# The output group's products in another order, and one product's weights summed ten half slabs sooner

## The chip, the cores and the metric

The kernel runs on one core of a Trainium2 chip. The metric is the device time of one execution in microseconds (us). It is given as the median of several runs; beside them one execution was taken by the hardware profiler, and every duration below is from that one. Engines are named as the profile names them: PE is TensorE, PEld its weight loads, ACT ScalarE, DVE VectorE, POOL GpSimd, SP SyncE.

## The reference, cut to what matters

Two layers over 256 tokens and a model width of 2048, all in fp32. Each layer normalises, projects into four branches (sparse attention, retention, a gated recurrence, attention into a memory), multiplies each branch's output by a gate, sums the four, and projects the sum with `w_out` into the residual:

```python
def hybrid_layer(x, mem, norm_g, w_in, qk_g, ...):
    h = rms_norm(x, norm_g)
    u = h @ w_in
    ...
    merged = jnp.zeros_like(x)
    for n, (y, z) in enumerate(((y_a, a_z), (y_b, b_z), (y_c, c_z), (y_m, m_z))):
        branch = y.reshape(B, S, W).astype(dt) * jax.nn.silu(z)
        merged = merged + jax.nn.sigmoid(gate_all[:, :, n]) * (branch @ w_branch[n])
    return x + merged @ w_out
```

The change concerns the last product, `merged @ w_out`, of the second layer: 256 x 2048 by 2048 x 2048. It is called the output group below.

## The kernel before

**Matrix products in parts.** Each fp32 operand is split into a high and a low part in a format that TensorE takes at full rate, and a product is made of three: high by high, high by low, low by high. Names that end in h and l are such parts (mg0h, mg0l); `whi` and `wlo` are those of the weights. A matmul of the GEMMs is 128 x 128 by 128 x 512, recorded at L145 for all of them; the other operations of ACT, DVE and POOL are recorded at L127, so the lines of the profile go by tile names.

**Weight slabs.** Weights come in slabs of 1 MB (128 x 2048), which SP loads into `raw` (four buffers; `load`, L420). Each slab is cut into two half slabs: `cut_piece` makes `whi` with a cast on ACT and then `wlo` with a subtraction on DVE. There are four buffers of such pairs, so the cuts run four half slabs ahead of PE: each time PE has been given the matmuls of one half slab, `advance` cuts another, and first sends what is due for later ones. An ordinary half slab of an output block feeds 12 matmuls.

**The merged rows.** `merged` is held in four column blocks acc0 to acc3. Each is turned by a transpose on DVE and 16 small DMAs (`mgp<-mgpi`), which POOL and SP issue in turns; those of acc1, which comes last, are all on POOL. Then ACT and DVE make mg0h and mg0l, and so on. The blocks are done in the order 0, 3, 2, 1 (`MERGED`), which are blocks 0, 1, 2, 3 of the output group.

**The output group of the last layer.** `w_out` is taken in four column chunks of 512. Chunks 0 and 1 are made block by block (tile `wo`): (c, b) in `LAST_ORDER` is block b of chunk c, one slab, two half slabs, 24 matmuls. Chunks 2 and 3 are made together, as a two by two scheme over both halves of rows and columns with seven products in place of eight (tile `px`). A plain number i in `LAST_ORDER` is such a product: four half slabs of 6 matmuls each. `last_take` makes one and `last_forms` makes the row combinations that four of them need: s3 for product 1, s1 for 3, s2 for 4, r4 for 0 (each is split into h and l on ACT and DVE). Products 2, 5 and 6 take merged rows as they are.

The weights of products 0 and 5 are raw slabs. Those of the others are sums of blocks of `w_out`, which DMAs make: a first block is loaded by SP (`last_block`, L494), and further ones are added onto it by accumulating DMAs that POOL issues. There are two chains of four half slabs. Chain y (`sumy`) serves products 2, 3, 4 and 6 one after another: as a half slab has been cut for one product, the next block is added onto it for the next (`LAST_NEXT`). Chain x (`sumx`) serves product 1 alone: one load and one accumulate for each half slab. `LAST_BEGIN` says how many half slabs ahead of a product's first cut its loads and accumulates are sent, in units of `AHEAD` = 10; `last_product` in `gemm_plan` turns this into positions in the list of cuts, and `split_weights` sends them when the cuts come to that position.

**What sets the order.** Each engine works through its instructions in the order in which the program issues them, and that order comes from the list of cuts: the combinations, casts and copies are tasks that get their turns between cuts. POOL's and SP's DMA queues have eight completion lanes each, so that a DMA waits for the one eight before it on its queue.

Of the kernel before, what the change touches and what calls it, by code (L numbers as in the profile page):

```python
# [154 lines left out]
DUO, AHEAD, FIRST, MERGED = (2, 0, 3, 1), 10, 0, (0, 3, 2, 1)  # L155
# [1 line left out]
STAGES = ((False, 1, 1), (True, 0, 1), (False, 0, 0), (True, 0, 1), (True, 1, 1))  # L157
LAST_SUM, RING, EARLY = (True, 1, 0), 5, 8
BETWEEN_PRODUCTS = (4, 3, 4, 4, 3, 2, 3)
LAST_ORDER = ((0, 0), (1, 0), (0, 1), (1, 1), 2, (0, 2), 1, (1, 2), 3, (0, 3), 4, 0, (1, 3), 5, 6)  # L160
LAST_RAW, LAST_NEXT = {0: (1, 1), 5: (1, 0)}, {2: (True, 0, 1), 3: (True, 1, 1), 4: (True, 1, 0)}
LAST_BEGIN = {2: ((AHEAD, "y", (False, 0, 0)),), 1: ((2 * AHEAD, "x", (False, 0, 1)), (AHEAD, "x", (True, 1, 1)))}
MOVES, STEPS, BANKS, WARM = 5, 2, 2, 7
MARGIN, LATE = 500.0, 2500.0

# [123 lines left out]
def gemm_plan(wmem, win, wbr, wout):  # L289
# [22 lines left out]
    def last_product(l, i, part):  # L312
# [3 lines left out]
        if not part:  # L316
            for ahead, chain, stage in LAST_BEGIN.get(i, ()):
                begins[len(cuts) - ahead] = chain, stage
# [5 lines left out]
    for l in range(L):  # L324
# [18 lines left out]
        if l + 1 < L:  # L343
# [3 lines left out]
            continue  # L347
        for at in LAST_ORDER:
            if isinstance(at, tuple):
# [14 lines left out]
def trunk(ctx: ExitStack, tc: tile.TileContext, x, xt, memt, ng, qkg, hg, lbl, win, wmem, wbr, wout,  # L364
# [1251 lines left out]

    for at in LAST_ORDER:
        if isinstance(at, tuple):
# [61 lines left out]
```

## Time and profile before

| what | us |
|---|---|
| median of 3 runs | 1836.58 |
| the runs | 1834.44, 1836.58, 1836.6 |
| the profiled execution | 1835.12 |
| its span, first to last instruction | 1833.3 |
| PE busy in the span | 1801.6 |
| DVE, ACT, POOL busy in the span | 1369.4, 1077.8, 400.6 |

The profiled execution lies 1.5 below the median of the runs, and its span 1.8 below its own time. The output group begins at 1716.04 us of the span with block (0, 0), and PE's last matmul ends about 10 us before the span does.

How to read the rows: a row of the timeline has the start in us from the span's start, the busy time, the engine, the line, the operation, the tile written, the tiles read, their shape, how many instructions the row joins (x4), and in brackets how long the engine was idle before it and what ended that. For a DMA row on POOL or SP the time is that of the issue; when a transfer lands is in the chain of waits, which gives issue and duration until landing, and in the views by tile. A row of the view by windows gives for a stretch each engine's busy time and number of instructions, the granted TensorE clock (1.00 is full speed), the busy share of the DMA engines and GB/s.

### The profile page before, as it was taken

What the parts mean: (1) busy time and instruction counts of PE and PEld (TensorE: products, weight loads), DVE (VectorE), ACT (ScalarE), POOL (GpSimd) and SP (SyncE); (2) the same over time, 40 slices, a digit from 0 to 9 for tenths busy, and PEclk for the clock granted to TensorE, in tenths of its full rate; (3) what the DMA queues carried; (4) which work ended last, traced back from release to release, by engine and by line L of the source; (5) the groups of instructions that cost most, each with busy time, mean ns of one, the idle gap of its engine ahead of it and who ended that gap; (6) DMA issues with size and microseconds to landing.
All of it is one profiled execution on the core that took longest, in us unless ns stands there. A gap on an engine that the chain in (4) does not pass through costs nothing.

```text
span 1833.3 us, 24392 instructions
## 1 busy us (share of the span) xinstructions
PE 1801.6 (98%) x8812; PEld 1497.3 (82%) x8812; DVE 1369.4 (75%) x1482; ACT 1077.8 (59%) x1283; POOL 400.6 (22%) x599
## 2 busy tenths in 40 slices
PE   9999999999999999999999999999999999999976
PEld 8889888888888888888888888888888888888854
DVE  5667798787878677777566698787877868677665
ACT  5756665456767656564466656545666755655453
POOL 0022420033332110103231340004322211111320
PEclk9999999999999999999999999999999999999988
DMA  8769965689999899977785985669999999996986
GB/s 333 267 208 307 276 213 197 235 240 266 282 268 285 258 237 284 248 236 240 244 273 184 308 238 194 225 227 258 258 287 249 290 257 270 261 247 226 300 192 167
DMA packets 127401, 459.84 MB, mean 251 GB/s; under 512 B 23472, under 2 KB 44720, under 8 KB 95024
## 3 DMA queue, kind: packets, MB, share of 16 engines
q1 hardware_dynamic: 89200, 356.14, 55.6%
q0 software_dynamic: 37792, 101.88, 28.7%
q8 instruction: 69, 1.13, 0.2%
q14 instruction: 52, 0.43, 0.1%
q10 hardware_dynamic: 288, 0.26, 0.0%
HBM read 428.05 MB, written 6.29 MB: 237 GB/s over the span
## 4 chain that ended last, share of the span: by engine, by line
PE 94%; DMA 4%; DVE 0%; ACT 0%; issue 0%; SPq 0%; POOL 0%; ACTq 0%; POOLq 0%
PE u L145 50%; PE px L145 22%; PE bw L145 9%; PE wo L145 6%; PE mv L145 2%; PE mk L145 2%; DMA sumy<-in_wout 1%; DMA mgp<-mgpi 1%; DMA raw<-in_wout 1%; PE ixrp L145 0%; PE mov L145 0%; PE mlg L145 0%; PE co L145 0%; PE bo L145 0%; PE aov L145 0%
## 5 line engine op out<-in xcount | busy, mean ns | idle before, releaser
L127 DVE TENSOR_TENSOR wlo<-raw,whi 128x1024 fp32r<-128x1024 f32 (+3 forms) x548 | 645.2, 1186 | 314.3 <-ACT whi L127 309.3
L127 ACT CAST whi<-raw 128x1024 fp32r<-128x1024 f32 (+3 forms) x548 | 559.3, 1024 | 536.7 <-PE u L145 339.3
L127 DVE TENSOR_TENSOR wlo<-sum,whi 128x1024 fp32r<-128x1024 f32 x240 | 288.0, 1220 | 63.8 <-ACT whi L127 57.1
L127 ACT CAST whi<-sum 128x1024 fp32r<-128x1024 f32 x240 | 250.5, 1053 | 101.2 <-PE px L145 50.7
L127 POOL DMA_DIRECT2D sum<-in_win x152 | 137.3, 910 | 609.3 <-DVE wlo L127 575.1
L127 POOL DMA_DIRECT2D mgp<-mgpi x72 | 38.4, 549 | 152.1 <-issue 94.0
L145 PE MATMUL u<-whi,x11h 128*128 128x512 f32 (+2 forms) x176 | 67.5, 384 | 0.0
L145 PE MATMUL u<-whi,x01h 128*128 128x512 f32 (+2 forms) x176 | 67.5, 384 | 0.0
L145 PE MATMUL u<-whi,x02h 128*128 128x512 f32 (+2 forms) x176 | 67.5, 383 | 0.0
L145 PE MATMUL u<-whi,x12h 128*128 128x512 f32 (+2 forms) x176 | 67.4, 383 | 0.0
L145 PE MATMUL u<-whi,x00h 128*128 128x512 f32 (+2 forms) x176 | 67.4, 383 | 0.0
L145 PE MATMUL u<-whi,x10h 128*128 128x512 f32 (+2 forms) x176 | 67.4, 383 | 0.0
L145 PE MATMUL u<-whi,x13h 128*128 128x512 f32 (+2 forms) x176 | 67.2, 382 | 0.0
L145 PE MATMUL u<-whi,x03h 128*128 128x512 f32 (+2 forms) x176 | 67.1, 381 | 0.0
L145 PE MATMUL u<-wlo,x11h 128*128 128x512 f32 (+2 forms) x176 | 67.1, 381 | 0.0
L145 PE MATMUL u<-wlo,x01h 128*128 128x512 f32 (+2 forms) x176 | 67.1, 381 | 0.0
L145 PE MATMUL u<-wlo,x00h 128*128 128x512 f32 (+2 forms) x176 | 67.1, 381 | 0.0
L145 PE MATMUL u<-wlo,x02h 128*128 128x512 f32 (+2 forms) x176 | 67.1, 381 | 0.0
L145 PE MATMUL u<-whi,x10l 128*128 128x512 f32 (+2 forms) x176 | 67.1, 381 | 0.0
L145 PE MATMUL u<-wlo,x12h 128*128 128x512 f32 (+2 forms) x176 | 67.0, 381 | 0.0
L145 PE MATMUL u<-wlo,x03h 128*128 128x512 f32 (+2 forms) x176 | 67.0, 381 | 0.0
L145 PE MATMUL u<-wlo,x10h 128*128 128x512 f32 (+2 forms) x176 | 67.0, 381 | 0.0
(536 smaller groups left out, 4594.9 us busy)
## 6 DMA issues: line engine op xcount, KB each, us to landing
raw<-in_win SPq DMA_DIRECT2D x180, 1024.0 KB, 6.6
sum<-in_win POOLq DMA_DIRECT2D x152, 512.0 KB, 8.6
sum<-in_win SPq DMA_DIRECT2D x80, 512.0 KB, 6.9
raw<-in_wbr SPq DMA_DIRECT2D x32, 1024.0 KB, 6.9
raw<-in_wout SPq DMA_DIRECT2D x28, 1024.0 KB, 6.7
raw<-in_wmem SPq DMA_DIRECT2D x12, 1024.0 KB, 5.3
sumy<-in_wout POOLq DMA_DIRECT2D x12, 512.0 KB, 10.4
raw<-in_win SPq DMA_DIRECT2D x8, 656.0 KB, 4.3
```

Of the source, the lines that this page charges most:

```text
L127: return call(*args, **kw)
L145: return self.engine.matmul(out, w, x, **kw)
```

## The change

Two lines differ. `LAST_ORDER` puts product 2 ahead of block (1, 1) and product 3 ahead of block (1, 2); from product 4 on it is as before. Between products 2 and 3 of chain y stand (1, 1), (0, 2) and product 1, where (0, 2), product 1 and (1, 2) stood; between 3 and 4 stand (1, 2) and (0, 3), where (0, 3) stood alone. `LAST_BEGIN` sends the loads of chain x 30 half slabs ahead of product 1's first cut in place of 20, and the accumulates 20 ahead in place of 10.

```diff
-LAST_ORDER = ((0, 0), (1, 0), (0, 1), (1, 1), 2, (0, 2), 1, (1, 2), 3, (0, 3), 4, 0, (1, 3), 5, 6)
+LAST_ORDER = ((0, 0), (1, 0), (0, 1), 2, (1, 1), (0, 2), 1, 3, (1, 2), (0, 3), 4, 0, (1, 3), 5, 6)
 LAST_RAW, LAST_NEXT = {0: (1, 1), 5: (1, 0)}, {2: (True, 0, 1), 3: (True, 1, 1), 4: (True, 1, 0)}
-LAST_BEGIN = {2: ((AHEAD, "y", (False, 0, 0)),), 1: ((2 * AHEAD, "x", (False, 0, 1)), (AHEAD, "x", (True, 1, 1)))}
+LAST_BEGIN = {2: ((AHEAD, "y", (False, 0, 0)),), 1: ((3 * AHEAD, "x", (False, 0, 1)), (2 * AHEAD, "x", (True, 1, 1)))}
```

On the engines this moves the following. POOL's queue, from the last of the earlier sums to the end of the output group's accumulates (`mgp<-mgpi` are the transposes of the merged rows, eight for each of acc0, acc3 and acc2 and sixteen for acc1; `sumx` and `sumy` are the accumulates of the two chains):

```order
 L127 DMA sum<-in_win 128x1024 x32
-L127 DMA mgp<-mgpi 32x2x128 x28
+L127 DMA mgp<-mgpi 32x2x128 x2
 L127 DMA sumx<-in_wout 128x1024 x4
-L127 DMA mgp<-mgpi 32x2x128 x12
-L127 DMA sumy<-in_wout 128x1024 x12
+L127 DMA mgp<-mgpi 32x2x128 x36
+L127 DMA sumy<-in_wout 128x1024
+L127 DMA mgp<-mgpi 32x2x128 x2
+L127 DMA sumy<-in_wout 128x1024 x11
```

The four accumulates of chain x stood behind 28 of the 40 transposes, among acc1's; they stand now behind the first two of acc0's. The first accumulate of chain y stands ahead of the last two of acc1's.

ACT from mg3h on, before (s3h is the combination for product 1, `us` the copy of product 2's result; `whi<-raw` and `whi<-sumy` are cuts):

```order
L127 CAST mg3h<-mgp 128x1024
L127 CAST whi<-raw 128x1024 x3
L127 CAST s3h<-r_14522 128x1024
L127 CAST whi<-sumy 128x1024 x2
L127 CAST mg2h<-mgp 128x1024
L127 CAST mg1h<-mgp 128x1024
```

and in the changed kernel:

```order
L127 CAST mg3h<-mgp 128x1024
L127 CAST whi<-raw 128x1024
L127 CAST whi<-sumy 128x1024 x2
L127 CAST s3h<-r_14522 128x1024
L127 CAST whi<-sumy 128x1024 x2
L127 CAST whi<-raw 128x1024
L127 CAST mg2h<-mgp 128x1024
L127 CAST whi<-raw 128x1024 x3
L127 COPY us<-px 128x512
L127 CAST mg1h<-mgp 128x1024
```

Between mg3h and mg1h stood five cuts; now there are nine and the copy of product 2's result.

ACT at the cuts of product 0 and the cast of its combination r4h, before:

```order
L127 CAST whi<-sumy 128x1024 x2
L127 COPY xc<-wo 128x512 x2
L127 CAST whi<-raw 128x1024
L127 CAST r4h<-r_14522 128x1024
L127 CAST whi<-raw 128x1024 x7
```

and in the changed kernel:

```order
L127 CAST whi<-sumy 128x1024 x3
L127 COPY xc<-wo 128x512 x2
L127 CAST whi<-raw 128x1024 x4
L127 CAST r4h<-r_14522 128x1024
L127 CAST whi<-raw 128x1024 x4
```

DVE at the same place, where r4l stood ahead of the sum of product 4's result into `us` and now stands behind it:

```order
-L127 TENSOR_TENSOR wlo<-raw,whi 128x1024 x3
+L127 TENSOR_TENSOR wlo<-raw,whi 128x1024
+L127 TENSOR_TENSOR r_14522<-s_14656,mgp 128x512
+L127 TENSOR_TENSOR wlo<-raw,whi 128x1024 x3
+L127 TENSOR_TENSOR us<-us,px 128x512
 L127 TENSOR_TENSOR r4l<-r_14522,r4h 128x1024
-L127 TENSOR_TENSOR wlo<-raw,whi 128x1024
-L127 TENSOR_TENSOR us<-us,px 128x512
 L127 TENSOR_TENSOR wlo<-raw,whi 128x1024 x4
```

All four cuts of product 0's slabs stand ahead of r4h and r4l now, where one (ACT) and three (DVE) did.

## The prediction

> **What bounds the kernel now.** I read the page first, then the waits and the timeline of PE, and from each stall of PE backwards to the engine and the queue that ended it. The page:
>
> ```profile
> span 1833.3 us, 24392 instructions
> PE 1801.6 (98%) x8812; PEld 1497.3 (82%) x8812; DVE 1369.4 (75%) x1482; ACT 1077.8 (59%) x1283; POOL 400.6 (22%) x599
> PE 94%; DMA 4%; DVE 0%; ACT 0%; issue 0%; SPq 0%; POOL 0%; ACTq 0%; POOLq 0%
> ```
>
> TensorE is busy 98% of the span and holds 94% of the chain that ended last; the 4% of DMA in that chain are places where PE stood. So the change, which takes no matmul away, can only be worth what PE loses. Where PE loses, by stretches (the columns are us, PE busy, PEld, DVE, ACT, POOL, PEclk, DMA share, GB/s):
>
> ```profile
> 1660.00:1737.80 77.80, 77.80 (x345) 64.42 (x344) 56.42 (x49) 37.70 (x40) 21.72 (x38) 1.00 0.81 251
> 1807.00:1823.10 16.10, 16.07 (x71) 12.96 (x70) 13.61 (x14) 7.67 (x8) 0.77 (x1) 1.00 0.22 83
> ```
>
> Up to 1737.8 and from 1807 PE is never idle, and the clock is whole. A matmul takes 16.10/71 = 0.2268 us from start to start. All that PE loses in the stages that the change touches lies between these two stretches; its timeline there:
>
> ```profile
> 1740.29 0.39 PE L145 MATMUL px<-whi,mg0l 128*128 128x512 f32 x1
> 1753.71 0.79 PE L145 MATMUL px<-whi,mg3h 128*128 128x512 f32 x1 [13.04 <-ACT whi L127]
> 1759.15 0.39 PE L145 MATMUL px<-wlo,mg3h 128*128 128x512 f32 x1
> ...
> 1790.83 0.39 PE L145 MATMUL px<-whi,s2l 128*128 128x512 f32 x1
> 1792.51 0.51 PE L145 MATMUL px<-whi,s2h 128*128 128x512 f32 x1 [1.29 <-ACT whi L127]
> 1794.11 0.40 PE L145 MATMUL px<-whi,s2l 128*128 128x512 f32 x1
> 1799.85 0.64 PE L145 MATMUL px<-whi,r4l 128*128 128x512 f32 x1 [3.66 <-DVE r4l L127]
> 1803.61 0.39 PE L145 MATMUL px<-whi,r4l 128*128 128x512 f32 x1
> ```
>
> **Stall 1.** From 1740.29 to 1759.15 PE makes 11 steps, worth 2.5 us, in 18.86: 16.4 lost, the slow clock after the wait included. **Stall 2.** From 1790.83 to 1803.61 it makes 18 steps, worth 4.1, in 12.78: 8.7 lost. Of these, 2.6 fall between 1790.83 and 1794.11 (3 steps in 3.28), at the last half slab of product 4; the other 6.1 at product 0's merged rows r4, of which 1.5 are the slow clock (10 steps in 3.76 from 1799.85 on). Together 25.1.
>
> What ended stall 1 was a cut of weights (`whi`) on ACT. ACT works in order, so I look at what it stood at, and at POOL's queue behind that:
>
> ```profile
> 1751.67 1.04 ACT L127 CAST mg1h<-mgp 128x1024 fp32r<-128x1024 f32 x1 [17.07 <-DMA mgp<-mgpi]
> ...
> 1724.91 3.62 POOL L127 DMA_DIRECT2D sumx<-in_wout  x4
> 1736.84 0.53 POOL L127 DMA_DIRECT2D mgp<-mgpi  x1 [5.58 <-DMA sumx<-in_wout]
> 1741.84 0.53 POOL L127 DMA_DIRECT2D mgp<-mgpi  x1 [4.47 <-DMA sumx<-in_wout]
> 1747.13 0.53 POOL L127 DMA_DIRECT2D mgp<-mgpi  x1 [4.76 <-DMA sumx<-in_wout]
> 1747.99 2.24 POOL L127 DMA_DIRECT2D mgp<-mgpi  x4 [0.32 <-DMA mgp<-mgpi]
> ```
>
> ACT stood 17.07 us at the cast of mg1h, and the cuts that PE needed stood behind it. mg1h waited for the 16 transposing DMAs of acc1, the last block of the merged rows, all on POOL, and POOL was held three times by sumx accumulates that it had issued four in a row: each DMA of that queue waits for the one eight before it, and the accumulates landed some 5 us apart. Stall 2:
>
> ```profile
> 1778.85 12.47 DMA sumy<-in_wout
> ...
> 1791.41 1.04 ACT L127 CAST whi<-sumy 128x1024 fp32r<-128x1024 f32 x1 [3.69 <-DMA sumy<-in_wout]
> 1794.26 1.06 ACT L127 CAST r4h<-r 128x1024 fp32r<-128x1024 f32 x1
> 1798.58 1.22 DVE L127 TENSOR_TENSOR r4l<-r,r4h 128x1024 fp32r<-128x1024 f32 x1
> ```
>
> The last accumulate of chain y was issued at 1778.85 and took 12.47 us; its cut came late, and r4h and r4l, which stand behind it on ACT and DVE, came later still.
>
> **The change, part by part.** No matmul, cut, cast or DMA is added or taken away.
>
> *The x chain, ten half slabs sooner.* On SP the four first loads of sumx, and on POOL the four accumulates, move ahead of work that they stood behind. What they pass, from the timelines of SP and POOL, with the landing times of sumx's DMAs (the tile's view) and those of the raw slabs (the page):
>
> ```profile
> 1664.18 0.33 SPq L420 DMA_DIRECT2D raw<-in_win  x1
> 1672.34 0.33 SPq L420 DMA_DIRECT2D raw<-in_wbr  x1
> 1693.74 2.05 SPq L494 DMA_DIRECT2D sumx<-in_wout  x4
> ...
> 1685.85 4.30 POOL L127 DMA_DIRECT2D mgp<-mgpi  x8 [43.15 <-issue]
> 1695.31 4.21 POOL L127 DMA_DIRECT2D mgp<-mgpi  x8 [5.16 <-DVE mgpi L127]
> ...
> DMA to landing us min/median/max: 5.4/8.7/20.2
> ...
> raw<-in_wbr SPq DMA_DIRECT2D x32, 1024.0 KB, 6.9
> ```
>
> On SP the loads now follow the raw slab of 1664.18. SP next issues at 1672.34, so 2 MB go into a gap of 8 us; at the 251 GB/s of the first window row they take 8.4. The raw slabs behind them can slip by under a microsecond. A slab takes 6.9 us to land and is sent for four slabs, some 21 us of PE, ahead of its buffer's next cut, so PE feels nothing. On POOL the accumulates stand behind the first two of acc0's eight transposes, so they are issued at about 1687 (their first loads are then long there) and block nothing of acc1 any more. Its rows should land at about 1738, 13 us sooner, and mg1h, which moreover stands behind four cuts more, no longer holds PE: **−16.4**.
>
> What is late next are the rows that the accumulates now precede. The first lands 5.4 us after its issue, the shortest that the tile's view has, and the others 5.0 to 5.3 apart, as the POOL rows of stall 1 were: about 1692.5, 1697.5, 1702.5 and 1708. The last of acc0's rows wait, eight back, for the first two accumulates and share the queue with the others, so they land by 1708 to 1710.5. Needed:
>
> ```profile
> 1709.54 1.06 ACT L127 CAST mg0h<-mgp 128x1024 fp32r<-128x1024 f32 x1 [0.41 <-DMA mgp<-mgpi]
> 1711.76 1.26 ACT L127 ACTIVATE gate<-u,rs1r 128x512 f32<-128x512 f32 x2
> 1716.04 0.39 PE L145 MATMUL wo<-whi,mg0h 128*128 128x512 f32 x1
> 1724.23 1.05 ACT L127 CAST mg3h<-mgp 128x1024 fp32r<-128x1024 f32 x1 [4.21 <-DMA mgp<-mgpi]
> 1726.92 0.39 PE L145 MATMUL wo<-whi,mg3h 128*128 128x512 f32 x1
> ```
>
> From mg0h's cast to the first output matmul ACT has the cast (1.06), a cut (1.05) and the gates (1.26), about 3.3 us, so the rows may land until 1712.7: spare 2 to 5 us. acc3's rows come after the last accumulate, by 1722 at the latest where SP's own half of them lies behind the sumy loads as before; mg3h started at 1724.23 for a matmul at 1726.92, so it gets no later. I take **0**, between a gain of 0 (PE lost nothing here) and a loss of 2.
>
> *Products further apart, chain y.* Between products 3 and 4 stand two blocks instead of one, 24 matmuls or 5.44 us more for the accumulates of product 4. Without stall 1 the last one is issued at 1778.85 − 16.4 − 5.4 = 1757; at the same 12.47 it lands at 1769.5. It was 2.6 late at 1791.31, so it would do until 1788.7 − 16.4 = 1772.3. Spare 2.8: **−2.6**, and nothing in place of it (range 0 to 2.6, the lateness itself).
>
> *r4, in another place.* The cast r4h before stood behind one raw cut of product 0's slabs, now behind all four, as the order rows of ACT and DVE show. Weight buffers hold four half slabs, so the fourth cut can't begin before PE has ended product 4; call the moment when product 0 is due X. The cast of the cut begins 0.2 after X (a matmul lasts 0.39 and the next is due after 0.2268), takes 1.05, then r4h 1.06: PE's first matmul of product 0 starts about X + 2.2. DVE makes that cut's low half (1.23, one handoff behind), the copy-out sum of product 4 and r4l:
>
> ```profile
> 1799.71 1.22 DVE L127 TENSOR_TENSOR wlo<-raw,whi 128x1024 fp32r<-128x1024 f32 x1
> 1800.85 0.68 DVE L127 TENSOR_TENSOR us<-us,px 128x512 f32<-128x512 f32 x1
> ```
>
> 0.2 + 1.05 + 1.23 + 0.68 + 1.22 with four handoffs of about 0.05 is X + 4.6. The third matmul, the first that reads r4l, was due at X + 0.45: PE loses **4.1** here in place of 6.1. Bounds: 3.6, if the operations overlap by 0.1 each as rows 1799.71 and 1800.85 do and the matmul's end frees the buffer at once; 4.8, if `us` waits another half microsecond for product 4's last matmul to drain.
>
> Whether the clock halves again is open. The granted clock behind the two long waits, by windows:
>
> ```profile
> 1745.50:1759.00 13.50, 4.63 (x10) 3.39 (x11) 6.25 (x6) 5.88 (x6) 6.26 (x9) 0.50 0.67 128
> 1800.10:1803.40 3.30, 3.30 (x9) 2.51 (x9) 1.95 (x3) 1.04 (x1) 0.00 (x0) 0.50 1.03 303
> ```
>
> It was 0.50 behind idle times of 13.04 and 3.66 us; behind 1.29 there is no sign of it (the matmul of 1792.51 takes 0.51, not 0.64). The new idle is about 2.2 and 1.9, with two matmuls between. The Trainium skill, "TensorE: Matmul & The Clock Gate", section "What's actually happening", says that the clock goes cold after an idle window of about 3.4 us which runs freely; by that rule it does not halve here, and the trace's three cases agree. If two short idle times counted as one long, the sum would be 1.5 higher, as in stall 2. I take 0 and keep 1.5 for the range.
>
> *Tail.* After product 0 the order of both kernels is the same, and PE has no idle from 1807 on: 0.
>
> **Sum**, against the profiled execution, 1835.12 us (span 1833.3 and 1.8 around it): 1835.12 − 16.4 − 8.7 + 4.1 = 1814.1. The median of the runs, 1836.58, is 1.5 above that execution: forecast **1815.6**.
>
> **Rivals.**
>
> *The stall moves to acc0 (A).* The accumulates ahead of acc0's rows take longer than 5 us each: with the tile's median of 8.7 from issue to landing, one after another, the last lands at 1687 + 35 = 1722 and the rows at 1724, 11 late: 1827. For it: four accumulates did hold POOL 15 us in all before. Against: raw loads are no denser in 1687 to 1709 than they were in 1725 to 1747, where they came 5 us apart. Range 1818 to 1827; chance 0.13.
>
> *Chain y stays late (B).* Stall 1 goes, but the 5.4 us are eaten, for instance as the accumulates are held by DVE's cuts: 2.6 and the halved clock 1.5 return: 1819.7. Chance 0.07.
>
> *Slower (C).* As A, but every accumulate takes the 12.47 that one of chain y took: 1687 + 50 + 2 = 1739 for acc0's rows, 26 late, where the stalls that go are worth 21: 1842. It decides from about 12.1 us each on (21 + 3.7 late). Against it: nothing in the trace has four in a row at that pace. Chance 0.04.
>
> *That the change doesn't do what it says* is out: the order rows show the accumulates of sumx ahead of 38 transposes, and chain y's products moved.
>
> **How the numbers follow.** Forecast 1815.6 with 0.76; A 0.13, B 0.07, C 0.04. The forecast's own bounds: down 0.5 for r4 and 2.1 for the spread of the runs (1834.44 to 1836.6), so 1813; up 0.7 for r4, 1.5 for the clock, 2.6 for y, 2 for mg0, so 1822.4. That takes in B and half of A; I set 1812 to 1823. Measurement tells 0.2% (3.7 us) from no change: faster means under 1832.9, which all but C give, and a little of A's far end might not: faster 0.94, same 0.02, slower 0.04.
>
> **What would show it.** In the profile of the changed kernel: no PE idle above 1 us between 1737 and product 0; sumx accumulates issued at 1687 and landing by 1709; mg0h before 1712.7; mg1h with no wait on its transposes that PE sees; the last accumulate of product 4 landing before 1772; two idle spells of 2.2 and 1.9 at r4h and r4l with full clock behind them. It is wrong if mg0h starts after 1713 (A, C), if a sumy cut ends a wait of PE at product 4 (B), or if PEclk shows 0.50 behind r4.

## The result, and the profile after

The changed kernel takes 1819.72 us (median of 4 runs, 1819.13 to 1821.62); the kernel before took 1836.51 beside it (median of 4, 1834.44 to 1836.6). The ratio of the two is 0.9913, 95% interval 0.9896 to 0.993: 16.8 us faster, where 21.0 were forecast. Its profiled execution took 1821.62 us, the slowest of the four. The page and PE's waits in the output group:

```profile
span 1819.9 us, 24386 instructions
PE 1799.6 (99%) x8812; PEld 1495.5 (82%) x8812; DVE 1369.0 (75%) x1482; ACT 1077.7 (59%) x1283; POOL 400.7 (22%) x599
...
PE px L145 <- DVE r4l L127: 2.2, 1, 2.2
PE px L145 <- ACT r4h L127: 2.1, 1, 2.1
PE wo L145 <- ACT mg3h L127: 1.8, 1, 1.8
PE wo L145 <- DVE mg3l L127: 0.5, 1, 0.5
```

The waits of 13.04 us for a cut, and those for chain y's cut, are gone. Two places are left: r4, as forecast, and the rows mg3, which the forecast had in time. PE's timeline there, with the output group's first matmul ahead of it:

```profile
1718.08 0.39 PE L145 MATMUL wo<-whi,mg0h 128*128 128x512 f32 x1
...
1728.74 0.39 PE L145 MATMUL wo<-whi,mg0l 128*128 128x512 f32 x1
1730.90 0.50 PE L145 MATMUL wo<-whi,mg3h 128*128 128x512 f32 x1 [1.78 <-ACT mg3h L127]
1732.16 0.50 PE L145 MATMUL wo<-whi,mg3l 128*128 128x512 f32 x1 [0.53 <-DVE mg3l L127]
1732.50 0.40 PE L145 MATMUL wo<-whi,mg3h 128*128 128x512 f32 x1
...
1780.73 0.39 PE L145 MATMUL px<-whi,s2l 128*128 128x512 f32 x1
1783.20 0.50 PE L145 MATMUL px<-whi,r4h 128*128 128x512 f32 x1 [2.08 <-ACT r4h L127]
1786.12 0.80 PE L145 MATMUL px<-whi,r4l 128*128 128x512 f32 x1 [2.19 <-DVE r4l L127]
1789.80 0.39 PE L145 MATMUL px<-whi,r4l 128*128 128x512 f32 x1
```

From 1728.74 to 1732.50 PE makes 4 steps (0.9 us) in 3.76: 2.85 lost at mg3. From 1780.73 to 1789.80 it makes 12 steps (2.7) in 9.07: 6.35 lost at r4, of which 1.6 are a slow clock behind the second wait. Between the two it loses nothing. That is 9.2 in place of 25.1. The output group begins at 1718.08, in the execution before at 1716.04: 2.0 us of this execution's time lie ahead of everything that the change touches (SP is already 2.04 later at the raw slab behind which the loads of chain x now stand), and the other three runs are 1.7 to 2.5 shorter.

What made mg3h late, from the timelines of POOL and ACT:

```profile
1689.06 3.66 POOL L127 DMA_DIRECT2D sumx<-in_wout  x4
1697.46 0.54 POOL L127 DMA_DIRECT2D mgp<-mgpi  x1 [2.54 <-DMA sumx<-in_wout]
1709.19 4.23 POOL L127 DMA_DIRECT2D mgp<-mgpi  x8 [2.18 <-DMA sumx<-in_wout]
...
1714.10 1.05 ACT L127 CAST mg0h<-mgp 128x1024 fp32r<-128x1024 f32 x1 [2.92 <-DMA mgp<-mgpi]
1724.93 1.05 ACT L127 CAST whi<-raw 128x1024 fp32r<-128x1024 f32 x1 [5.59 <-DMA raw<-in_wout]
1729.81 1.04 ACT L127 CAST mg3h<-mgp 128x1024 fp32r<-128x1024 f32 x1 [3.83 <-DMA mgp<-mgpi]
1744.35 1.05 ACT L127 CAST mg1h<-mgp 128x1024 fp32r<-128x1024 f32 x1
```

POOL's accumulates were done by 1709, and mg1h no longer waits for any transfer. But ACT now waits 5.59 us for a raw slab and 3.83 more for mg3's rows. The slab and half of the rows come by SP's queue; POOL's half of the rows was issued by 1713.4. The median times from issue to landing of what was issued between 1688 and 1716 us, in the kernel before:

```profile
raw<-in_wout SPq DMA_DIRECT2D x4, 1024.0 KB, 8.0
mgp<-mgpi SPq DMA_DIRECT2D x17, 32.0 KB, 7.3
```

and in the changed kernel:

```profile
raw<-in_wout SPq DMA_DIRECT2D x3, 1024.0 KB, 11.1
sumx<-in_wout POOLq DMA_DIRECT2D x4, 512.0 KB, 14.1
mgp<-mgpi SPq DMA_DIRECT2D x12, 32.0 KB, 11.3
```

In this stretch SP's slabs are 3 us slower and SP's share of the transposes, which stand between the slabs, 4 us. POOL's transposes of the same size are not (6.0 us before, 5.8 now). SP also issues later, as it waits for the transfer eight before: from 1690 to 1730 us it stood 8.7 us at slabs ahead of its transposes, against 4.6 before, and the last transpose of acc3 was issued at 1721.86, against 1714.74 (2.0 of that is this execution's later start). What is new in the stretch are the four accumulates; the four plain loads of chain x, which stood there before, are gone from it, so that fewer bytes were moved (7.40 MB against 8.50). That the accumulates are the cause is tested below.

### The profile page after: what moved, and what is told of

It reads as the page before. It is cut to its first block, busy times and chain, and to the rows that moved or that the text cites. A ratio compares the mean times of both kernels' runs of the same rounds, so it can differ in the third digit from the quotient of the medians.

```text
span 1819.9 us, 24386 instructions
## 1 busy us (share of the span) xinstructions
PE 1799.6 (99%) x8812; PEld 1495.5 (82%) x8812; DVE 1369.0 (75%) x1482; ACT 1077.7 (59%) x1283; POOL 400.7 (22%) x599
## 4 chain that ended last, share of the span: by engine, by line
PE 91%; DMA 4%; DVE 2%; issue 1%; ACT 1%; POOL 0%; SPq 0%; ACTq 0%; DVEq 0%; POOLq 0%
PE u L145 49%; PE px L145 21%; PE bw L145 9%; PE wo L145 5%; PE mv L145 2%; PE mk L145 2%; DMA sumy<-in_wout 1%; DMA mgp<-mgpi 1%; DVE wlo L127 1%; DMA raw<-in_wbr 1%; PE ixrp L145 0%; ACT whi L127 0%; PE mov L145 0%; PE mlg L145 0%; PE bo L145 0%
## 5 line engine op out<-in xcount | busy, mean ns | idle before, releaser
L145 PE MATMUL u<-wlo,x13h 128*128 128x512 f32 (+2 forms) x176 | 67.1, 381 | 0.0
```

The costliest lines, as they stand in the source:

```text
L145: return self.engine.matmul(out, w, x, **kw)
```

## The experiments

The first four tell apart which part of the change did what, and test r4 and mg3. Each ratio is to the kernel before, run beside that experiment (its medians are 1835.92 to 1836.69), with its 95% interval in brackets.

**The sums alone.** The old order of steps, the new `LAST_BEGIN`:

```diff
-LAST_ORDER = ((0, 0), (1, 0), (0, 1), 2, (1, 1), (0, 2), 1, 3, (1, 2), (0, 3), 4, 0, (1, 3), 5, 6)
+LAST_ORDER = ((0, 0), (1, 0), (0, 1), (1, 1), 2, (0, 2), 1, (1, 2), 3, (0, 3), 4, 0, (1, 3), 5, 6)
```

> The old order of steps, chain x ten half slabs sooner. Theory S (the sooner sums free POOL for acc1's transposes, and that alone ends stall 1): acc1's rows land before 1740, stall 1 (16.4 us) is gone, mg3h comes some 2.8 us late as in the changed kernel, stall 2 stays whole (8.7): 1836.5 - 16.4 + 2.8 = 1823. Rival O (the longer run of cuts ahead of mg1h in the new order ends stall 1): ACT still holds PE at mg1h, 1830 or more.

Measured: 1825.62 us (median of 4, 1823.53 to 1828.21), ratio 0.9944 (0.9929 to 0.9958). The waits of PE and the casts on ACT:

```profile
PE px L145 <- DVE r4l L127: 3.7, 1, 3.7
PE wo L145 <- ACT mg3h L127: 2.7, 1, 2.7
...
1744.24 1.05 ACT L127 CAST mg1h<-mgp 128x1024 fp32r<-128x1024 f32 x1 [3.56 <-DMA mgp<-mgpi]
```

ACT stands 3.56 us at mg1h in place of 17.07, and PE loses about 1.4 behind it. mg3h is late again, and stall 2 is whole (r4l 3.7 as before). Theory S holds in the main: the sooner sums take away 15.0 of stall 1's 16.4 us by themselves. But acc1's rows came at 1744 and not before 1740, and the last 1.4 are gone only with the new order, which puts four more cuts ahead of mg1h. The profiled execution, 1828.21, is the slowest of the four: in it mg3 cost 5.4 us and stall 2 10.5, each with a slow clock behind it.

**The order alone.** The new order, the old `LAST_BEGIN`:

```diff
-LAST_BEGIN = {2: ((AHEAD, "y", (False, 0, 0)),), 1: ((3 * AHEAD, "x", (False, 0, 1)), (2 * AHEAD, "x", (True, 1, 1)))}
+LAST_BEGIN = {2: ((AHEAD, "y", (False, 0, 0)),), 1: ((2 * AHEAD, "x", (False, 0, 1)), (AHEAD, "x", (True, 1, 1)))}
```

> The new order of steps, chain x sent as before. Theory S alone: acc1's transposes are held by the accumulates of chain x as before, their rows land at about 1751 and stall 1 keeps most of its 16.4 us; 2.6 go with chain y: about 1832 to 1834. Rival O: mg1h stands behind four more cuts and a copy, so PE has four more half slabs to go on with and would need mg1h only by about 1749: a stall of 2 to 4 us is left, mg3h is not late, r4 costs 6.3: 1836.5 - 25.1 + 3 + 6.3 = about 1821, so either part would have done nearly the whole.

Measured: 1831.1 us (median of 9, 1828.06 to 1832.71), ratio 0.9976 (0.9966 to 0.9986). ACT and PE:

```profile
1754.81 1.04 ACT L127 CAST mg1h<-mgp 128x1024 fp32r<-128x1024 f32 x1 [16.12 <-DMA mgp<-mgpi]
...
1756.85 0.79 PE L145 MATMUL px<-whi,s3h 128*128 128x512 f32 x1 [8.85 <-ACT whi L127]
```

ACT stands at mg1h nearly as long as before (16.12 us), and the stall moves from product 2's cuts to product 1's. The cuts ahead of mg1h last PE some 7 us longer (to its matmul of 1747.61, not 1740.29), about as rival O said; but mg1h's rows came at 1754 and not at 1751. Their last two transposes now stand behind the first accumulate of chain y and took 4.9 us to land (median), where the last four took 1.8 before. So PE is idle for 8.85 us in place of 13.04, and stall 1 keeps 12.6 of its 16.4. Theory S is the nearer one. The profiled execution is the fastest of the nine, 3.0 below their median. Alone the order is worth about 5 us, the sums 10, and both together 17.

**r4 between the halves of product 4.** In `last_take` of the changed kernel:

```diff
         product(to, form, part, i != 5, i in LAST_RAW)
+        if i == 4 and not part:
+            stream.until(last_ready, lambda: "r4" in last_made)
```

> The changed kernel with the combination r4 made and cast between the two halves of product 4, so that r4h and r4l stand behind two raw cuts of product 0 in place of four. Theory R (the 6.3 us lost at product 0 in the changed kernel are r4h and r4l standing behind cuts that wait for PE's end of product 4, with some 1.6 us of halved clock behind them): PE idles under 0.5 us there and the clock stays whole: 1819.7 - 6.3 = 1813.4. Rival Y (chain y's last cut, which lay only 0.4 us behind the moment when its buffer came free, is the bound, or the two raw cuts that are moved behind r4 come late): PE loses 2 us or more at product 4 or at product 0's later half slabs: 1815.5 to 1818.

Measured: 1820.62 us (median of 4, 1818.6 to 1821.78), ratio 0.9915 (0.99 to 0.9929): no gain on the changed kernel. PE's waits at r4, and a new place behind it:

```profile
1781.71 0.50 PE L145 MATMUL px<-whi,r4h 128*128 128x512 f32 x1 [0.55 <-ACT r4h L127]
1782.97 0.51 PE L145 MATMUL px<-whi,r4l 128*128 128x512 f32 x1 [0.52 <-DVE r4l L127]
1796.74 0.50 PE L145 MATMUL px<-whi,mg1h 128*128 128x512 f32 x1 [0.28 <-ACT whi L127]
1798.00 0.50 PE L145 MATMUL px<-wlo,mg1h 128*128 128x512 f32 x1 [0.76 <-DVE wlo L127]
```

The wait at r4 falls from 4.3 us to 1.1, and the clock behind it stays whole, as theory R had it: PE loses 1.7 us there in place of 6.4. But the time does not follow: PE now loses 2.35 at cuts in products 5 and 6. ACT stood 5.76 us ahead of them at the last raw slab, whose landing time stands in the view of DMA issues:

```profile
raw<-in_wout SPq DMA_DIRECT2D x1, 1024.0 KB, 13.8
```

Rival Y was right that something stands behind r4, wrong about what. The rest of the gain went elsewhere: mg3 cost 4.2 us in this execution, a slow clock included, in place of 2.85, and the stretch from the start of PE's last matmul to the end of the span was 0.7 longer (11.7 in place of 11.0).

**Chain x another ten half slabs sooner**, in the changed kernel:

```diff
-1: ((3 * AHEAD, "x", (False, 0, 1)), (2 * AHEAD, "x", (True, 1, 1)))}
+1: ((4 * AHEAD, "x", (False, 0, 1)), (3 * AHEAD, "x", (True, 1, 1)))}
```

> The changed kernel with chain x sent another ten half slabs sooner: loads 40 ahead and accumulates 30 ahead, so that these lie ahead of all transposes of the merged rows. Theory D (the accumulates, landing beside the raw slabs at 1697 to 1709, slowed SP's slabs and with them SP's share of acc3's transposes, which made mg3h late): mg3h is in time, PE loses nothing before product 0: 1819.7 - 2.8 = 1817. Rival L (SP's loads of chain y and its eight lanes make mg3h late whatever chain x does): mg3h late as before, 1819.7. Against both: the accumulates may hold up an earlier group's work at 1640 to 1685, then PE idles there and the time is above 1820.

Measured: 1817.46 us (median of 4, 1816.57 to 1818.4), ratio 0.9899 (0.9884 to 0.9913). PE's waits from 1600 us on, and the landing times between 1688 and 1716:

```profile
PE px L145 <- ACT r4h L127: 2.1, 1, 2.1
PE px L145 <- DVE r4l L127: 1.8, 1, 1.8
...
raw<-in_wout SPq DMA_DIRECT2D x5, 1024.0 KB, 6.3
mgp<-mgpi SPq DMA_DIRECT2D x21, 32.0 KB, 5.6
```

With the accumulates out of this stretch SP's transposes land in 5.6 us in place of 11.3, mg3h is in time and PE loses nothing until r4. Theory D holds. Loads and accumulates moved together here, but the loads lay ahead of this stretch in the changed kernel too (SP issued them at 1666.60). The run with the order alone is the counterpart: there the four loads stand in the stretch and the accumulates do not, slabs took 7.9 us and SP's transposes 7.7, and PE did not wait at mg3. Why an accumulate costs the others more than a load of the same 512 KB was not tried.

**Both at once**, the early r4 and the sums 40 and 30 ahead.

> Chain x 40 and 30 half slabs ahead and r4 between the halves of product 4, both at once. Theory W (r4's stall hides a second wait behind it: the last raw slab, that of block (1, 3), took 13.8 us to land where the accumulates of chain y and three residual transfers share the DMA engines, so that PE waits for its cut once r4 is in time): of the 7.1 us that were left with the sooner sums, r4 keeps about 1.6 and the last slab takes about 2.3: 1817.5 - 7.1 + 3.9 = 1814.3. Rival R (r4 was the last stall and the waits behind it in the earlier run came from its late mg3h): 1817.5 - 5.5 = 1812. Rival N (the stall is worth nothing, because the end is set by DMA): 1817.5.

Measured: 1815.85 us (median of 4, 1815.63 to 1816.88), ratio 0.989 (0.9876 to 0.9905). ACT at the last slab's cuts:

```profile
1792.23 2.00 ACT L127 CAST whi<-raw 128x1024 fp32r<-128x1024 f32 x2 [4.77 <-DMA raw<-in_wout]
```

ACT waits for the last slab and PE behind it, though only 1.3 us; r4 keeps 3.7, as the clock is slow again behind it. Theory W has the direction; the time is 1.6 us above what it gave. It misnamed the slab: PE makes block (1, 3) without a wait, and what it waits for is the second slab of product 5, whose matmuls with mg1h are the first to stand.

**The residual loads behind the last slab**, on top of both:

```diff
             ac.copy(got["us"][:, 1, :], to)
-            got["xc"] = residual(2)
...
             ac.copy(got["qs"][:, 0, :], to)
+            got["xc"] = residual(2)
...
+            if b == 3 and c:
+                ends[c] = added(c)
             open_chunks[c] = gemms(...)
-            if b == 2 and c:
-                ends[c] = added(c)
-            elif b == 3:
+            if b == 3:
```

> As the run before, with the two residual loads of SP (512 KB each) moved behind the last raw slab on SP's queue. Theory W: the last slab lands 2 us or more sooner (under 12 us from its issue), PE no longer waits for its cut, and the time is 1.5 to 2.5 below that of the run before: 1812 to 1813. Rival: the slab is held by chain y's accumulates and not by the residual loads; it lands within 1 us of before and the time is that of the run before. Against both: the residuals land too late for the sums of the last chunks and the tail grows by 1 or more.

Measured: 1812.72 us (median of 4, 1812.47 to 1813.36), ratio 0.9873 (0.9858 to 0.9888). The last raw slab, issue to landing, in the run before and in this one:

```profile
raw<-in_wout SPq DMA_DIRECT2D x1, 1024.0 KB, 14.4
```

```profile
raw<-in_wout SPq DMA_DIRECT2D x1, 1024.0 KB, 8.7
```

5.7 us sooner, and neither ACT nor PE waits for it any more. Theory W holds. The medians lie 3.1 us apart, the two profiled executions 4.4. Of these the traces give 1.3 to this wait and 1.2 to the stretch from PE's last matmul to the end of the span, which falls from 11.9 to 10.7; another 2.1 lie at r4, where r4h came half a microsecond sooner and no slow clock followed. Whether that also comes from the moved loads was not told apart.

**The residual loads alone**, with r4 where the change has it (and the sums 40 and 30 ahead).

> The kernel with chain x 40 and 30 ahead and with the late residual loads, but r4 where the change has it. If the wait for the last raw slab lies hidden behind r4's stall, moving the residuals alone is worth nothing: 1817.5, as with chain x alone. If DMA sets the end by itself, it is worth the 3.1 us that it gave behind the early r4: 1814.4.

Measured: 1817.33 us (median of 4, 1816.57 to 1817.6), ratio 0.9893 (0.9877 to 0.991): the time of the sums alone, 1817.46. While r4 stalls PE, the late slab is free. The early r4 alone is worth 1.6 us (between the medians, 1817.46 and 1815.85), the late residuals alone nothing, and both together 4.7: r4's stall hides the slab's.

**r4 ahead of all four cuts**, on top of the late residuals: the line of the third experiment, put before product 4's first half in place of behind it.

> As the run with late residuals, with r4 made and cast ahead of all four raw cuts of product 0 (before product 4 begins) in place of behind two. Theory R: the 1.6 us that PE still lost at r4h and r4l go, and nothing else waits: 1812.7 - 1.6 = 1811.1. Rival: the two sums that make r4 now stand ahead of a low half that product 4 needs, and PE loses 1 or more at product 4: 1812.5 to 1814.

Measured: 1807.94 us (median of 4, 1807.66 to 1808.71), ratio 0.9844 (0.983 to 0.9859), the fastest kernel of this study, 3.2 us below what was expected. But not for the reason given: PE still loses 1.7 us in all. What moved is the end, and that was luck. DVE, and SP's last store, with late residuals and r4 behind two cuts:

```profile
1792.99 4.62 DVE L127 TENSOR_TENSOR wlo<-sumy,whi 128x1024 fp32r<-128x1024 f32 x4
...
1798.13 1.22 DVE L127 TENSOR_TENSOR us<-qs,us 128x1024 f32<-128x1024 f32 x1
...
1806.27 0.58 SPq L1566 DMA_DIRECT2D out<-us  x1
```

and with r4 ahead of all cuts:

```profile
1792.33 1.22 DVE L127 TENSOR_TENSOR us<-qs,us 128x1024 f32<-128x1024 f32 x1
1793.47 4.62 DVE L127 TENSOR_TENSOR wlo<-sumy,whi 128x1024 fp32r<-128x1024 f32 x4
...
1801.43 0.59 SPq L1566 DMA_DIRECT2D out<-us  x1
```

The task that makes the last output column got its turn sooner: its sum (`us<-qs,us`) stood behind four low halves on DVE and stands now ahead of them, so that the residual is added and the column stored 4.8 us earlier. PE's last matmul starts at the same time in both, within 0.2 us.

**The changed kernel once more.**

> The changed kernel as it is, once more, for a second profile beside these. If mg3h's lateness belongs to the kernel and not to one execution, PE loses 2 to 4 us there again and 6 to 6.5 at r4, and the time is 1819 to 1821.

Measured: 1821.26 us (median of 4, 1820.07 to 1822.1), ratio 0.992 (0.9904 to 0.9937). PE waits 2.0 us at mg3 and 3.9 at r4 again, so both belong to the kernel. The 2.0 us ahead of the output group do not: it begins at 1715.84 here. This time the clock fell behind mg3 too, so that mg3 cost 4.2 (the window behind the wait; PEclk is the number before the last two):

```profile
1729.60:1733.00 3.40, 3.39 (x8) 2.67 (x9) 3.40 (x5) 1.53 (x2) 1.03 (x3) 0.53 1.08 255
```

## Why the prediction was right, and where it was wrong

The direction, the mechanism and the main term were right, and the time lay in the range: 1819.72 for a forecast of 1815.6. What it missed lies at mg3, at r4l and in the clock, 5.0 us on the profiled execution. The time stayed within the range partly by luck: mg3's loss is more than the 2 that the range held for late rows, while the 2.6 that it held for chain y were not needed.

*Stall 1, −16.4: right.* The accumulates of chain x had held acc1's transposes; issued sooner, they no longer do. The run with the sums alone shows that this part of the change carries 15.0 of it. The rows themselves came later than worked out: the last transposes of acc1 were issued at 1735.87 and took about 7.4 us, so they landed at 1743 to 1744, on the clock of before about 1741.5, for a forecast of 1738. The four cuts more and the copy ahead of mg1h covered that.

*Chain y, −2.6: right, with less to spare.* No wait for a cut of chain y is left. The step gave the last accumulate 2.8 us of spare at a landing time of 12.47. It took 13.6 (1762.36 to 1776.0), so that ACT waited for it, but not so long that PE did:

```profile
1776.10 1.05 ACT L127 CAST whi<-sumy 128x1024 fp32r<-128x1024 f32 x1 [2.06 <-DMA sumy<-in_wout]
```

*mg0: right; mg3: the step that failed.* The prediction said of mg3h that "it gets no later" and took 0, at most 2, for the rows behind the accumulates. It looked at POOL's queue, and there the last landing came as worked out: the last accumulate by 1709, which is 1707 on the clock of before, for a forecast of 1708 (the first three came 2 to 3 us later than forecast). mg0h started 2.9 us after ACT was ready for it, and PE did not feel it. But half of the transposes go by SP, between raw slabs, and the step let those slabs "slip by under a microsecond": it priced the four loads, and there it was right (SP's issues up to 1693.42 keep the 2.04 us by which this execution was later anyway), but not the four accumulates that share the DMA engines with the slabs behind them. Slabs took 11.1 us in place of 8.0, mg3h came at 1729.81, and PE lost 2.85. The run with the accumulates 30 ahead takes this away.

*r4: right in kind, too small.* r4h's wait was worked out as 2.2 and measured as 2.24 (from 1780.96, when product 0 was due, to 1783.20). r4l was forecast at 4.6 behind that moment and came at 5.16, since DVE had more queued than the one low half of the sum:

```profile
1780.85 3.49 DVE L127 TENSOR_TENSOR wlo<-raw,whi 128x1024 fp32r<-128x1024 f32 x3
1784.25 0.68 DVE L127 TENSOR_TENSOR us<-us,px 128x512 f32<-128x512 f32 x1
1784.85 1.22 DVE L127 TENSOR_TENSOR r4l<-r,r4h 128x1024 fp32r<-128x1024 f32 x1
```

ACT had come late to the first of product 0's cuts, behind chain y's last cut and two copies, so that three low halves stood in a row: 0.6 us.

*The clock: taken as 0, measured as 1.6.* The window behind r4 in the changed kernel:

```profile
1786.20:1789.50 3.30, 3.30 (x8) 2.63 (x9) 0.15 (x1) 1.04 (x1) 0.00 (x0) 0.52 1.05 246
```

Two waits of 2.08 and 2.19 us with two matmuls between were enough. The prediction had named this case and kept 1.5 for it in the range. The rule that the prediction weighed from the Trainium skill ("TensorE: Matmul & The Clock Gate", "What's actually happening"), a cold clock after an idle window of about 3.4 us, does not cover this: no single wait was that long, and the measurement decides.

Together on the profiled execution: 1814.1 + 2.85 (mg3) + 0.6 (r4l) + 1.6 (clock) = 1819.2, and 2.0 that lay ahead of the output group make 1821.2, for 1821.62 measured.

*The rivals.* Rival A named the place, the rows behind the accumulates, but the wrong queue and too high a price (mg3 by SP, 2.85; not acc0 by POOL, up to 11). B and C did not happen.

## What to carry to other kernels

When a transfer is moved out of a stall, look at every queue that shares the DMA engines where it goes to, and not only at the queue that it leaves: small transfers between large ones on a queue wait as long as the large ones do (here transposes of 32 KB took 7.3, 11.3 and 5.6 us where the slabs of 1 MB around them took 8.0, 11.1 and 6.3). A stall of the busiest engine hides what is late behind it, as r4's hid the last slab's, so waits next to each other should be taken away together before one of them is called worthless. And where tasks take turns, an edit can move an operation far from it: the largest gain on top of the change, 4.8 us, came from the last column's sum getting an earlier turn.

## What was not expected of the hardware

The TensorE clock fell after idle times well below the 3.66 us that had preceded it in the kernel before. Two waits of 1.0 and 0.5 us at r4, in the run with r4 early and the sums 40 ahead, were followed by a clock of 0.52:

```profile
PE px L145 <- ACT r4h L127: 1.0, 1, 1.0
PE px L145 <- DVE r4l L127: 0.5, 1, 0.5
...
1779.00:1782.40 3.40, 3.40 (x8) 2.69 (x9) 3.11 (x4) 1.60 (x2) 0.00 (x0) 0.52 1.04 244
```

But 1.78 and 0.53 at mg3 in the changed kernel were followed by a whole clock:

```profile
1732.50:1780.70 48.20, 48.20 (x213) 39.81 (x212) 40.20 (x39) 33.72 (x37) 13.13 (x16) 1.00 0.93 245
```

The same kind of wait (mg3h, then mg3l, 0.5) left the clock whole here, after 1.78 us at mg3h, but cost it in the second profile of the same kernel (0.53 after 1.46 us) and in the run with r4 early (0.52 after 1.52). So it can't be read from the length of the idle time alone. What decides it was not tried.
